# A float32 hybrid decoder layer: side transfers moved to the weights' queue, value blocks interleaved, PSUM banks tracked by the planner

## The chip, the cores and the metric

The kernel runs on one core of a Trainium2 chip. The metric is device time in microseconds (us), the median of three runs. The engines are named as in the profile: PE (TensorE, matmuls), PEld (its weight loads), DVE (VectorE), ACT (ScalarE), POOL (GpSimd) and SP (SyncE, which here only issues transfers). A q behind an engine's name (ACTq) is its sequencer: it issues transfers and waits, and stands in one line with the engine's own work.

## The reference

For 256 tokens of width 2048 the layer computes, in float32,

```python
h = rms_norm(x, norm_g)
proj = h @ dn_w_in                       # 2048 -> q, k, v, a/b gates, xq, z
q, k, v = silu(conv4(q)), silu(conv4(k)), silu(conv4(v))
mix = rms_norm(gated_delta_rule(l2(q), l2(k), v, g(a), sigmoid(b)))   # 24 value heads
xa  = softmax(rms_norm(xq) @ rms_norm(K).T / 16) @ V   # K, V = rms_norm(mem) @ mem_w_kv, 256 tokens
out = x + (concat(mix, xa) * silu(z)) @ w_out
```

The delta rule is done in chunks of 128 tokens here. For each chunk and head a unit lower triangular 128x128 matrix has to be inverted: `inverse` does the 32x32 diagonal blocks by substitution on DVE, `merge` joins them with small matmuls.

## The kernel before

**Weights.** All weight matrices come in 273 tiles of 128x1024 float32 (512 KB, named `st`, five buffers). Each is split into a rounded half `hi`, a cast on ACT (L261), and a rest `lo`, a subtraction on DVE (L263). The pair is a `wt` tile (four buffers), and every large product is done as hi*hi + hi*lo + lo*hi in the fast fp32r format. `wnext` traces transfer, cast and subtraction of one tile together; `wload` keeps `LOOK = 1` tile beyond the one in use.

**Products.** `proj_b` (tiles `pb`) makes 256x512 outputs from 8 or 16 weight tiles, in two PSUM banks, with 12 matmuls of 512 columns for each weight tile. `proj_a` (tiles `pa`) makes a 128-column block of projected features over 256 tokens from two weight tiles, one matmul of 512 and one of 256 columns for each of 16 k tiles. The eight PSUM banks are in groups: `pa` 2, `A` 2, `m` 2, `tr` 1, `B` 1.

**Order of the large work** (`PLAN`, L49 to 72): V0, V1 (values of the memory), K0, the gate columns `ab`, K1, then eight `x` blocks (queries of the cross-attention), `k` blocks with Z6 and Z7 (columns of z) between, Z0 to Z2, then for each of 12 head pairs a `q` and two `v` blocks with the remaining `k` and Z blocks between, and four output blocks `o`.

**Side work.** Everything else is written as Python generators. The program keeps a clock `now` that runs with the matmuls' estimated lengths, and resumes a generator when its estimated inputs are there: `mem_stats` and `tok_prep` (the two input norms; `tok_prep` makes the token tiles `hkt` that `ab` and everything from `x` on reads), `gates`, `decay`, `gram` (product `pkk`), `inverse`, `merge` (products `pm`), `delta` (`pkq`, `pvt`, `pU`, `pO`, `pqs`), `attend` (`xss`, `xsc`, `xpT`, `xo`) and `split_y` (transposes `pyT`). `calm` makes a generator wait while DVE has more than 0.8 us of estimated work. A scheduler then sorts the instructions of each engine again, by its own estimate of when each could start, with the traced order as priority. Nothing is pinned to the traced order. After that each engine is a strict queue.

**Transfers.** SP issues the weights, the inputs, the decay rows `erow` and the output. ACT issues what belongs to the inverses, through DRAM: each pair's matrix (`dN`), the diagonal blocks read back (`inN`), the inverted blocks written (`dY`, `dX`), and for each of six merges 6 loads into `XN` and 8 into `Y`. That is 84 loads of 16 KB for the six merges, and 27 more transfers.

**A finished product** of `proj_a` leaves its bank in two steps (`halves`, L309): ACT copies 256 columns, then DVE adds the other 256 from PSUM to them. A `Z` product is freed by the SiLU on ACT (`zs`).

Lines of helpers: L98 every side operation of DVE, ACT and POOL, L166 every matmul, L170 every transpose, L255 the weights' transfers.

Of the kernel before, what the change touches and what calls it, by code (L numbers as in the profile page):

```python
# [33 lines left out]
LOOK = 1  # L34
WARM = 7
XPACE = 1.5
HOP = 0.25
SLACK = 0.7
POLL = 0.3
CALM = 0.8  # L40
INV_CALM = 0.6
GATE_CALM = 0.8
# [6 lines left out]
PLAN = [("V", 0)] * 8 + [("V", 1)] * 8 + [("K", 0)] * 8 + [("ab", 0)] + [("K", 1)] * 8  # L49
# [30 lines left out]
def hybrid_kernel(ctx: ExitStack, tc: tile.TileContext, x, xT, memT, W, prm_d, cst_d, out):  # L80
    nc = tc.nc
    te, sy = nc.tensor, nc.sync
    now, fin = [0.0], [0.0]

    class Engine:
# [9 lines left out]
        def __getattr__(self, op):  # L95
            def call(*a, **k):
                self.run(self.cost(self, op, a, k))
                return getattr(self.eng, op)(*a, **k)  # L98
            return call
# [24 lines left out]
    po = Engine(nc.gpsimd, lambda e, op, a, k: 0.6)  # L124

# [33 lines left out]
    def mm(o_, lhsT, rhs, start, stop):  # L159
        n = 1  # L160
        for d in rhs.shape[1:]:
            n *= d
        if rhs.dtype == F32:
            n = 4 * max(n, 16)
        now[0] += n / 2400.0
        te.matmul(o_, lhsT, rhs, start=start, stop=stop)  # L166
# [59 lines left out]
    ahead = []  # L226
# [3 lines left out]
    def wnext():  # L230
        st = stp.tile([128, 1024], F32, name="st", tag="st")
        wt = wp.tile([128, 2, 1024], F32R, name="wt", tag="wt")
        hi, lo, src = wt[:, 0, :], wt[:, 1, :], st
        kind, t = PLAN[wpos[0]]
        if kind == "Z":
# [5 lines left out]
            hi, lo = [h.rearrange("p (k t c) -> p k t c", k=2, t=4) for h in (hi, lo)]  # L241
            src = st.rearrange("p (t k c) -> p k t c", t=4, k=2)
            dst = st.rearrange("p (t c) -> p t c", t=4)
        else:
            data, dst = W[plain[0]], st
            plain[0] += 1
        if kind == "ab":

            v = wt.rearrange("p a (k c) -> p (a k c)", c=64).rearrange("p (k a c) -> p k a c", a=2, c=64)
            hi, lo, src = v[:, :, 0, :], v[:, :, 1, :], st.rearrange("p (k c) -> p k c", c=64)  # L250
        parts = 2 if wpos[0] == 0 else 1
        dma[0] = max(dma[0], free.pop(0)) + 1.46
        for a in range(parts):
            w = slice(a * 1024 // parts, (a + 1) * 1024 // parts)
            sy.dma_start(dst[:, w] if parts > 1 else dst, data[:, w] if parts > 1 else data)  # L255
            if parts > 1:
                if a == 0:
                    sy.dma_start(prm[:, 0:P_CW], prm_d[:, 0:P_CW])
                mem_load(a, 1)
            se.run(0.95 / parts, dma[0] + 2.0)  # L260
            se.eng.copy(hi[:, w] if parts > 1 else hi, st[:, w] if parts > 1 else src)  # L261
            ve.run(1.14 / parts, se.end)
            ve.eng.tensor_tensor(out=lo[:, w] if parts > 1 else lo, in0=st[:, w] if parts > 1 else src,  # L263
                                 in1=hi[:, w] if parts > 1 else hi, op=ALU.subtract)
# [44 lines left out]
    def halves(dst, pt):  # L309

        se.copy(dst, pt[:, 256:512])
        yield
        ve.tensor_tensor(out=dst, in0=pt[:, 0:256], in1=dst, op=ALU.add)
        yield

    def proj_b(steps, act, tag, done, before=None):

        pts = [PS(tag, "pb0"), PS(tag, "pb1")]
        n = len(steps)
        for s in range(0, n, 2):  # L320
# [8 lines left out]
            for i, (r, k2) in enumerate(rk):  # L329
# [902 lines left out]
```

## Time and profile before

| | |
|---|---|
| median of three runs | 889.41 us (887.72 to 889.97) |
| the profiled execution: its time, its span | 890.17 us, 888.4 us |
| PE busy | 870.1 us, 98% of the span |
| DVE, ACT busy | 636.3 us (72%), 524.8 us (59%) |
| granted TensorE clock, mean | 0.996 |
| HBM read | 158.14 MB, 186 GB/s over the span |

The span is what lies between the first and the last instruction; 1.77 us of the profiled execution's time lie around it. Busy time of ACT does not hold the time in which it issues or waits for transfers. In the timeline a row is: start, length, engine, line, operation, out<-in, shape, count, and in brackets the idle time of the engine before it with what ended it.

### The profile page before, as it was taken

The numbers are of one execution on the slowest core, as the hardware profiler recorded it, in microseconds if no ns is written. First come the engines' busy times: TensorE is split into PE (matmuls) and PEld (weight loads), VectorE is DVE, ScalarE is ACT, GpSimd is POOL, SyncE is SP. The second block draws the span as 40 slices with busy tenths as digits, with TensorE's granted clock in tenths as the row PEclk, the third lists the DMA queues.
The fourth block names the chain that finished last, engine by engine and source line by source line (L and its number), as shares of the span: only waits on it lengthen the run. The fifth ranks groups of instructions, "written<-read, shape, count | busy, mean of one in ns | idle before, by whom it ended". The sixth has DMA issues, their size and how long they took to land.

```text
span 888.4 us, 13971 instructions
## 1 busy us (share of the span) xinstructions
PE 870.1 (98%) x5091; PEld 732.1 (82%) x5091; DVE 636.3 (72%) x1275; ACT 524.8 (59%) x936; POOL 45.9 (5%) x62
## 2 busy tenths in 40 slices
PE   8998999999999999999999999999999999999998
PEld 5886888888877788887888888878888888888886
DVE  6779886668784899976679998852878765454442
ACT  7655555577665655536589976555866754333341
POOL 0000000101010000121000001100000000000000
PEclk9998999999999999999999999999999999999999
DMA  8963555566767675676636555653544546766560
GB/s 287 345 209 122 186 168 150 174 203 206 240 214 207 212 239 189 194 207 184 186 114 187 178 175 176 170 180 104 166 137 138 166 154 230 231 191 224 199 204 25
DMA packets 98637, 165.90 MB, mean 187 GB/s; under 512 B 24304, under 2 KB 64008, under 8 KB 98568
## 3 DMA queue, kind: packets, MB, share of 16 engines
q1 hardware_dynamic: 72816, 158.08, 55.2%
q10 hardware_dynamic: 25752, 6.93, 3.3%
q8 instruction: 40, 0.66, 0.3%
q14 instruction: 29, 0.24, 0.1%
HBM read 158.14 MB, written 6.84 MB: 186 GB/s over the span
## 4 chain that ended last, share of the span: by engine, by line
PE 81%; DVE 6%; DMA 4%; ACT 3%; issue 3%; POOL 1%; ACTq 1%; SPq 0%; DVEq 0%; POOLq 0%
PE pb L166 43%; PE pa L166 29%; PE pO L166 2%; DVE wt L263 2%; DMA st<-W_d 2%; PE pm L166 1%; ACT wt L261 1%; PE pU L166 1%; PE pkq L166 1%; DVE acc L98 1%; PE xsc L166 1%; DMA erow<-dgc 1%; DMA XN<-dX 1%; PE xo L166 1%; PE pyT L170 1%
## 5 line engine op out<-in xcount | busy, mean ns | idle before, releaser
L263 DVE TENSOR_TENSOR wt<-st,wt 128x1024 fp32r<-128x1024 f32 (+1 forms) x274 | 332.4, 1216 | 125.0 <-ACT wt L261 122.5
L261 ACT CAST wt<-st 128x1024 fp32r<-128x1024 f32 (+1 forms) x274 | 285.7, 1047 | 192.0 <-PE pb L166 127.2
L166 PE MATMUL pa<-hkt,wt 128*128 128x512 f32 (+1 forms) x1792 | 336.5, 342 | 1.5 <-DVE wt L263 1.3
L166 PEld LDWEIGHTS pa<-hkt,wt 128*128 128x128 f32 x1792 | 274.1, 188 | 40.0 <-DVE wt L263 1.4
L166 PE MATMUL pb<-wt,hkt 128*128 128x512 f32 x768 | 183.9, 394 | 4.3 <-ACT zs L98 2.2
L166 PEld LDWEIGHTS pb<-wt,hkt 128*128 128x128 f32 x768 | 141.5, 188 | 35.4 <-ACT zs L98 3.5
L166 PE MATMUL pb<-wt,yhi 128*128 128x512 f32 x512 | 158.6, 391 | 0.0
L166 PEld LDWEIGHTS pb<-wt,yhi 128*128 128x128 f32 x512 | 95.2, 188 | 19.2
L166 PE MATMUL pb<-wt,ylo 128*128 128x512 f32 x256 | 99.7, 390 | 0.0
L166 PE MATMUL pb<-wt,mkt 128*128 128x512 f32 x384 | 94.2, 403 | 2.4 <-ACT mkt L98 0.9
L166 PEld LDWEIGHTS pb<-wt,mkt 128*128 128x128 f32 x384 | 74.1, 195 | 20.7 <-DVE wt L263 2.2
L98 DVE SCALAR_TENSOR_TENSOR acc<-raw,prm,acc 128x255 f32<-128x255 f32 x144 | 68.9, 479 | 9.3 <-ACT acc L98 8.3
L166 PEld LDWEIGHTS pb<-wt,ylo 128*128 128x128 f32 x256 | 48.0, 188 | 10.2
L98 ACT COPY raw<-pa 128x256 f32<-128x256 f32 x48 | 17.9, 373 | 35.5 <-PE pa L166 31.8
L98 ACT ACT_TABLE_LOAD x29 | 37.2, 1283 | 1.2 <-DVE acc L98 0.7
L98 DVE TENSOR_SCALAR dec<-erow,gcc 128x128 f32<-128x128 f32 x96 | 23.0, 279 | 18.2 <-DMA erow<-dgc 18.2
L98 DVE TENSOR_TENSOR inT<-inXT,inN 96x1 f32<-96x1 f32 (+22 forms) x92 | 29.9, 341 | 0.3
L98 DVE TENSOR_REDUCE inXT<-inT 96x1 f32<-96x1 f32 (+22 forms) x92 | 29.1, 337 | 0.4
L98 ACT ACTIVATE acc<-raw,prm 128x256 f32<-128x256 f32 x48 | 24.4, 509 | 7.8 <-DMA Y<-dY 3.8
L98 POOL TENSOR_TENSOR e<-e,mhalf 128x4 f32<-128x4 f32 x12 | 13.5, 1123 | 270.9 <-DVE e L98 270.9
L98 POOL TENSOR_TENSOR srk<-skt,mhalf 128x2 f32<-128x2 f32 x12 | 12.4, 1032 | 221.4 <-DVE skt L98 221.4
L98 DVE TENSOR_TENSOR raw<-pa,raw 128x256 f32<-128x256 f32 x48 | 20.1, 418 | 4.6 <-ACT raw L98 4.3
(199 smaller groups left out, 698.8 us busy)
## 6 DMA issues: line engine op xcount, KB each, us to landing
st<-W_d SPq DMA_DIRECT2D x272, 512.0 KB, 4.2
erow<-dgc SPq DMA_DIRECT2D x24, 256.0 KB, 4.4
dN<-dec ACTq DMA_DIRECT2D x12, 256.0 KB, 2.6
xraw<-xT_d SPq DMA_DIRECT2D x8, 256.0 KB, 5.4
res<-x_d SPq DMA_DIRECT2D x8, 256.0 KB, 4.6
mst<-memT_d SPq DMA_DIRECT2D x7, 256.0 KB, 4.5
out_dram<-res SPq DMA_DIRECT2D x7, 256.0 KB, 5.3
inN<-dN ACTq DMA_DIRECT2D x4, 192.0 KB, 4.1
```

What stands on the lines that cost most here:

```text
L98: return getattr(self.eng, op)(*a, **k)
L166: te.matmul(o_, lhsT, rhs, start=start, stop=stop)
L170: te.transpose(o_, i_, ident)
L261: se.eng.copy(hi[:, w] if parts > 1 else hi, st[:, w] if parts > 1 else src)
L263: ve.eng.tensor_tensor(out=lo[:, w] if parts > 1 else lo, in0=st[:, w] if parts > 1 else src, in1=hi[:, w] if parts > 1 else hi, op=ALU.su ...
```

## The change

1. **Side transfers.** All the transfers that ACT issued (`se.dma_start`) go through SP (`sd.dma_start`). ACT keeps three, at the very start: two pieces of the memory and the parameters.
2. **Weights.** `wnext` is split. `wraw` traces transfers for as long as one of the five `st` buffers is free by the planner's clock; `wnext` casts and subtracts. `LOOK` is 2. The memory pieces have their own buffers and no longer share `st`.
3. **Order.** V0 and V1 alternate tile by tile, so that a memory k tile serves both; then K0, K1, and `ab` behind K1. Z7 takes four tiles each after k3 and k4.
4. **Banks.** `PS`, `give`, `spare`, `bank` keep when each PSUM bank is free by the planner's clock; generators and products wait for it there. Z1 moves from the banks `A` to `pa`, x0, x1 and K1 change groups too, `ab` takes `B`.
5. **`halves`** copies all 512 columns in one ACT instruction; DVE adds the halves in SBUF.
6. **Traced order.** While the planner's clock is under 45 us every instruction is pinned behind the one traced before it on its engine.
7. **Estimates.** Small matmuls and transposes get other lengths; the three limits of `calm` double; `tok_prep` and `mem_stats` start at 8 us of the planner's clock (24 and 12 before), with 3.0 us per piece (1.5 before).

```diff
-LOOK = 1
+LOOK = 2
+PINNED = 45.0
-CALM = 0.8
-INV_CALM = 0.6
+CALM = 1.6
+INV_CALM = 1.2
-PLAN = [("V", 0)] * 8 + [("V", 1)] * 8 + [("K", 0)] * 8 + [("ab", 0)] + [("K", 1)] * 8
+PLAN = [("V", 0), ("V", 1)] * 6 + [("V", 0)] * 2 + [("V", 1)] * 2
+PLAN += [("K", 0)] * 8 + [("K", 1)] * 8 + [("ab", 0)]
...
+    def pin(ins):
+        return tc.keep_in_program_order(ins) if PINNED is None or now[0] < PINNED else ins
...
+    class Transfers:
+        def dma_start(self, *a, **k):
+            fin[0] = max(fin[0], now[0] + 3.0)
+            return sy.dma_start(*a, **k)
+    sd = Transfers()
...
+    def spare(tag, n=1):
+        return sum(t <= now[0] for t in idle[tag]) >= n
+    def give(pt, t):
+        idle[held.pop(id(pt))[0]].append(t)
+    def bank(tag, name):
+        yield from until(lambda: spare(tag))
+        return PS(tag, name)
...
+    def wnext():
+        while wpos[0] < len(PLAN) and free:
+            wraw()
...
-    def halves(dst, pt):
-        se.copy(dst, pt[:, 256:512])
-        yield
-        ve.tensor_tensor(out=dst, in0=pt[:, 0:256], in1=dst, op=ALU.add)
+    def halves(pt):
+        raw = S2("raw", [2, 256])
+        se.copy(raw.rearrange("p a t -> p (a t)"), pt)
+        give(pt, se.end)
+        yield
+        ve.tensor_tensor(out=raw[:, 0, :], in0=raw[:, 0, :], in1=raw[:, 1, :], op=ALU.add)
...
+        if kt < 2:
+            ve.tensor_scalar(out=m[:, 0, :], in0=src, scalar1=g, scalar2=None, op0=ALU.mult)
+        else:
+            se.activation(m[:, 0, :], src, AF.Copy, scale=g)
...
-                    se.dma_start(ys[p2][b, :, b], tsp[k][:, s0 : s0 + 4])
+                    sd.dma_start(ys[p2][b, :, b], tsp[k][:, s0 : s0 + 4])
...
-            return proj_b(kts, x_act, "pa" if 3 <= t < 6 else "A", z_done(t))
+            return proj_b(kts, x_act, "pa" if t in (1, 3, 4, 5) else "A", z_done(t))
-    spawn(mem_stats(), 12.0)
-    spawn(tok_prep(), 24.0)
+    first_loads()
+    spawn(mem_stats(), 8.0)
+    spawn(tok_prep(), 8.0)
```

What this makes of the engines' queues is seen at four places. First DVE at the start of the program. Before, with `gqk` (a product of two parameters), `wt` the rest of the first weight tile's two parts, and `mkt` the first memory tiles:

```order
L98 MEMSET warm 128x256
L98 TENSOR_TENSOR gqk<-prm 128x2
L263 TENSOR_TENSOR wt<-st,wt 128x512
L98 SCALAR_TENSOR_TENSOR mkt<-mst,prm,mkt 128x256
L263 TENSOR_TENSOR wt<-st,wt 128x512
```

And now, on the same engine:

```order
L112 MEMSET warm 128x256
L112 TENSOR_SCALAR nA<-nA 24x1
L112 TENSOR_SCALAR mkt<-mst,prm 128x256
L112 SCALAR_TENSOR_TENSOR mkt<-mst,prm,mkt 128x256
L330 TENSOR_TENSOR wt<-st,wt 128x512
L112 TENSOR_SCALAR mkt<-mst,prm 128x256
L112 SCALAR_TENSOR_TENSOR mkt<-mst,prm,mkt 128x256
L330 TENSOR_TENSOR wt<-st,wt 128x512
```

DVE now makes the rounded half of the first two memory tiles too, and ahead of all that stands `nA`, a small operation of `gates` that is traced late, is not pinned, and has come to the front. On ACT its input stands behind the casts of both parts of the first weight tile:

```order
L306 DMA mst<-memT_d 128x256
L308 DMA prm<-prm_d 128x40
L306 DMA mst<-memT_d 128x256
L326 ACT_TABLE_LOAD
L326 CAST wt<-st 128x512 x2
L112 ACTIVATE nA<-prm 24x1
L112 ACTIVATE msq<-mst 128x512
```

Second, PE from K0's end to the first x block. Before, K0 ends in pb_541 and pb_542 and K1 begins in pb_840 and pb_841; `pk` are the transposes of K0:

```order
L166 MATMUL pb_542<-wt,mkt 128x512 x6
L166 MATMUL pab<-hkt,wt 128x512 x8
L170 MATMUL pk<-cst,kn 128x128 x4
L166 MATMUL pab<-hkt,wt 128x512 x4
L170 MATMUL pk<-cst,kn 128x128 x2
L166 MATMUL pb_840<-wt,mkt 128x512
L170 MATMUL pk<-cst,kn 128x128 x2
L166 MATMUL pb_840<-wt,mkt 128x512
```

And now, at K1's end (pb_736 and pb_760; the transposes of K0 stand inside K1):

```order
L95 MATMUL pb_736<-wt,mkt 128x512 x6
L95 MATMUL pb_760<-wt,mkt 128x512 x6
L95 MATMUL pab<-hkt,wt 128x512 x14
L95 MATMUL pa<-hkt,wt 128x512
L95 MATMUL pa<-hkt,wt 128x256
L95 MATMUL pab<-hkt,wt 128x512
```

The gate columns stand behind K1, and 14 of their 16 matmuls follow each other.

Third, the loads of the first merge. Before, on ACT, between casts of weights and evictions (raw, acc, kq belong to blocks of k):

```order
L98 DMA XN<-dX_106 32x4x32
L98 ACTIVATE acc<-raw,prm 128x256
L98 DMA XN<-dX_106 32x4x32 x3
L98 COPY raw<-pa 128x256
L98 DMA XN<-dX_106 32x4x32 x2
L98 DMA Y<-dY_104 32x4x32
L98 ACTIVATE kq<-acc 128x256
L98 DMA Y<-dY_104 32x4x32 x2
L98 DMA dN_103<-dec 128x4x128
L98 DMA Y<-dY_104 32x4x32 x5
L98 ACTIVATE acc<-raw,prm 128x256
L261 CAST wt<-st 128x1024 x3
```

And now, on SP, between transfers of weights:

```order
L95 DMA st<-W_d 128x1024 x13
L95 DMA dY_104<-inXT 96x512 x2
L95 DMA st<-W_d 128x1024
L95 DMA dX_106<-inN 96x512
L95 DMA st<-W_d 128x1024 x3
L95 DMA XN<-dX_106 32x4x32 x6
L95 DMA Y<-dY_104 32x4x32 x8
L95 DMA st<-W_d 128x1024 x2
```

ACT has none of these left; 14 loads stand between two weights on SP.

Fourth, the first `pm` products on PE. Before:

```order
L166 MATMUL pkk<-kq 128x128
L166 MATMUL pm<-Y,dec 32x32 x16
L166 MATMUL pb_3832<-wt,hkt 128x512
L166 MATMUL pb_3831<-wt,hkt 128x512 x2
L166 MATMUL pb_3832<-wt,hkt 128x512 x2
L166 MATMUL pb_3831<-wt,hkt 128x512 x3
```

And now:

```order
L95 MATMUL pm<-Y,dec 32x32
L95 MATMUL pa<-hkt,wt 128x512
L95 MATMUL pa<-hkt,wt 128x256
L95 MATMUL pa<-hkt,wt 128x512
L95 MATMUL pm<-Y,dec 32x32
L95 MATMUL pa<-hkt,wt 128x256
...
L95 MATMUL pm<-Y,dec 32x32 x13
```

The first merge stands earlier, among the blocks of k and v instead of a Z block, and its first products come one by one between large matmuls. Over the whole program the number of runs of `pm` on PE goes from 29 to 39; the numbers of matmuls of every kind stay what they were.

More of the change, by code (lines that the diff above doesn't have):

```diff
@@ new lines, in wraw, with first_loads @@
+        wpos[0] += 1
+        raws.append((n, kind, st, src, dma[0] + 2.0))
+    def first_loads():
+        mst[0] = S2("mst", [512])
+        for a in range(2):
+            w = slice(a * 256, (a + 1) * 256)
+            pin(nc.scalar.dma_start(mst[0][:, w], memT[0][:, w]))
+            if a == 0:
+                pin(nc.scalar.dma_start(prm[:, 0:P_CW], prm_d[:, 0:P_CW]))
+    def wnext():
+        while wpos[0] < len(PLAN) and free:
+            wraw()
+        n, kind, st, src, landed = raws.pop(0)
+        wt = wp.tile([128, 2, 1024], F32R, name="wt", tag="wt")
+        hi, lo = wt[:, 0, :], wt[:, 1, :]
+        if kind == "Z":
+            hi, lo = [h.rearrange("p (k t c) -> p k t c", k=2, t=4) for h in (hi, lo)]
@@ L247, in wnext @@
         if kind == "ab":
             v = wt.rearrange("p a (k c) -> p (a k c)", c=64).rearrange("p (k a c) -> p k a c", a=2, c=64)
-            hi, lo, src = v[:, :, 0, :], v[:, :, 1, :], st.rearrange("p (k c) -> p k c", c=64)
-        parts = 2 if wpos[0] == 0 else 1
-        dma[0] = max(dma[0], free.pop(0)) + 1.46
+            hi, lo = v[:, :, 0, :], v[:, :, 1, :]
+        parts = 2 if n == 0 else 1
         for a in range(parts):
             w = slice(a * 1024 // parts, (a + 1) * 1024 // parts)
[L255 to L264, printed above, removed]
+            se.run(0.06 + 0.87 / parts, landed)
+            pin(se.eng.copy(hi[:, w] if parts > 1 else hi, st[:, w] if parts > 1 else src))
@@ L271, in wload @@
     def wload():
-        while wpos[0] < len(PLAN) and len(ahead) <= LOOK:
+        while (raws or wpos[0] < len(PLAN)) and len(ahead) <= LOOK:
             wnext()
@@ L711, in attend @@
         ve.tensor_tensor(out=pTl, in0=pp, in1=pTh, op=ALU.subtract)
+        give(pp, ve.end)
         yield from pe_soon()
-        px = PS("m", "xo")
+        px = yield from bank("m", "xo")
         c0 = (hd % 2) * 256
@@ L761, in gram @@
         kq, d = KQ[p], dD[p]
-        pk = PS("m", "pkk")
+        pk = yield from bank("m", "pkk")
         for b in range(NB):
@@ L946, in split_y @@
             yield from until(lambda: yf[j] is not None)
-            pt = PS("m", "pyT")
+            pt = yield from bank("m", "pyT")
             for h in range(2):
@@ L999, in delta @@
         se.activation(q2, kq[:, 1, :], AF.Square)
-        pk = PS("m", "pkq")
+        pk = yield from bank("m", "pkq")
+        vt = yield from bank("tr", "pvt")
         kqf = kq.rearrange("d a t -> d (a t)")
@@ L1025, in delta @@
         ve.tensor_tensor(out=kcl, in0=pkv[:, 0:4:2, :], in1=kch, op=ALU.subtract)
+        give(pk, ve.end)
         yield from pe_soon()
-        A = PS("A", "pU0")
+        A = yield from bank("A", "pU0")
         for h in range(2):
```

225 lines of the change are left out of this document (136 added, 89 removed).

## The prediction

> **What bounds the kernel now.** I read the page first, then windows of the engines' busy time, the chain of waits, the timeline of PE and of ACT at each gap, and the groups by form.
>
> ```profile
> span 888.4 us, 13971 instructions
> PE 870.1 (98%) x5091; PEld 732.1 (82%) x5091; DVE 636.3 (72%) x1275; ACT 524.8 (59%) x936; POOL 45.9 (5%) x62
> DVE  6779886668784899976679998852878765454442
> ```
>
> PE is idle for 888.4 - 870.1 = 18.3 us in all. The change leaves every matmul in place, so it can gain only those 18.3 us and the places where PE is busy but slow. DVE is full (nines) around slices 15 to 17 and 23 to 26, where the inverses and the delta rule run. From the chain of waits and from windows:
>
> ```profile
> 744.26 140.15 PE pb L166 x618
> ```
>
> ```profile
> 0.00:24.00 24.00, 20.37 (x67) 13.51 (x68) 17.04 (x32) 19.19 (x34) 0.20 (x4) 1.00 0.82 287
> 80.00:90.00 10.00, 7.80 (x25) 5.73 (x26) 8.87 (x22) 3.48 (x10) 0.00 (x0) 0.66 0.15 49
> ```
>
> The last 140 us are dense: 140.15 / 618 = 0.227 us for a matmul of 512 columns. No edit touches them. In the first 24 us PE runs 67 matmuls, 7 of them to warm up; 60 x 0.227 = 13.6, so 10.4 us are lost there. At 80 to 90 us PE does 25, at a granted clock of 0.66. Between these and the end, PE's timeline shows where it stands still:
>
> ```profile
> 77.26 1.98 PE L166 MATMUL pab<-hkt,wt 128*128 128x512 f32 x8
> 80.39 0.83 PE L170 MATMUL pk<-cst,kn 128*128 128x128 f32 x4 [1.15 <-DVE kn L98]
> ...
> 83.76 1.22 PE L166 MATMUL pab<-hkt,wt 128*128 128x512 f32 x2 [1.80 <-DVE hkt L98]
> ...
> 87.33 3.92 PE L166 MATMUL pb<-wt,mkt 128*128 128x512 f32 x13
> 91.10 0.39 PE L166 MATMUL pab<-hkt,wt 128*128 128x512 f32 x1
> ...
> 253.98 1.20 PE L166 MATMUL pb<-wt,hkt 128*128 128x512 f32 x4 [1.49 <-ACT zs L98]
> 276.87 1.43 PE L166 MATMUL pb<-wt,hkt 128*128 128x512 f32 x5 [0.38 <-ACT zs L98]
> 300.29 0.97 PE L166 MATMUL pb<-wt,hkt 128*128 128x512 f32 x3 [0.38 <-ACT zs L98]
> 401.16 0.50 PE L166 MATMUL pb<-wt,hkt 128*128 128x512 f32 x1 [1.34 <-ACT wt L261]
> ...
> 621.53 0.48 PE L166 MATMUL pa<-hkt,wt 128*128 128x512 f32 x1
> 621.94 0.26 PE L166 MATMUL pm<-Am,XN 32*32 32x32 f32 x8
> ...
> 623.92 1.32 PE L166 MATMUL pa<-hkt,wt 128*128 128x256 f32 x6 [1.28 <-DVE wt L263]
> 645.16 1.06 PE L170 MATMUL pyT<-cst,o 128*128 128x128 f32 x8 [1.14 <-DVE ylo L98]
> 671.99 0.63 PE L170 MATMUL pyT<-cst,o 128*128 128x128 f32 x4 [0.73 <-DVE ylo L98]
> ```
>
> So there are five kinds of loss: the start, the gate columns that wait for token tiles, Z products that wait for a bank, weights split too late around the merges, and transposes that wait for a bank.
>
> **The change part by part.**
>
> *Start.* The rows of before:
>
> ```profile
> 3.51 0.62 ACT L261 CAST wt<-st 128x512 fp32r<-128x512 f32 x1 [1.50 <-DMA st<-W_d]
> 4.76 0.51 ACT L98 ACTIVATE mkt<-mst,prm 128x256 fp32r<-128x256 f32 x1 [0.63 <-DMA mst<-memT_d]
> 5.32 5.41 PE L166 MATMUL pb<-wt,mkt 128*128 128x512 f32 x12 [0.93 <-ACT mkt L98]
> 5.62 0.62 ACT L261 CAST wt<-st 128x512 fp32r<-128x512 f32 x1 [0.36 <-DMA st<-W_d]
> 6.27 0.69 DVE L263 TENSOR_TENSOR wt<-st,wt 128x512 fp32r<-128x512 f32 x1 [0.49 <-ACT wt L261]
> 16.99 0.18 ACT L98 ACTIVATE nA<-prm 24x1 f32<-24x1 f32 x1
> ```
>
> The memory now travels beside the first weights, and each of its k tiles serves two weight tiles, so DVE and ACT have half the memory work per weight tile and the stops after the first tile should go. But `nA` is first on DVE, and on ACT its input stands behind the second cast. I put the second half of the first weight tile at 4.3 us (5.62 - 0.36 = 5.26 before, with two transfers fewer ahead of it; an estimate). Then both casts end at 4.9, `nA` on ACT and DVE (0.18, taken for both) at 5.3, the first rounded memory tile (taken as the 0.51 that it takes on ACT) at 5.8, its rest as much later at 6.3, the weights' rest (0.69) at 7.0. The first matmul starts at 5.8 instead of 5.32, the second waits until 7.0, and the first tile ends between 11.1 and 12.0 us, by when PE comes to its full rate (12 matmuls in 5.41 us before: half rate). That is 11.1 to 12.0 less 12 x 0.227 = 8.4 to 9.3 lost instead of 10.4. **Gain 1.5** (ends: -1 if the clock comes later, 3.5 if `nA` costs nothing).
>
> *Gate columns.* From 77.26 to 87.33 us PE does 14 `pab`, 2 `pb` and 8 transposes: 16 x 0.227 + 1.06 (eight transposes at 645.16) = 4.7 of 10.1 us, 5.4 lost; the next 13 matmuls take 3.77 instead of 2.95, since the clock has dropped, 0.8 more. Now `ab` stands behind K1, eight weight tiles (22 us) later, and `tok_prep` starts earlier. What is late next: the last two token tiles stand on ACT behind K1's squares and a cast.
>
> ```profile
> L98 ACT ACTIVATE junk<-pb 128x256 f32<-128x256 f32 x8 | 3.0, 380 | 1.6 <-PE pb L166 1.6
> L98 DVE TENSOR_TENSOR hkt<-hf,hkt 128x256 fp32r<-128x256 f32 x16 | 6.0, 418 | 0.0
> ```
>
> After K1 ends these are two squares (0.76), a cast (1.05), two casts of `hkt` (taken as 0.8) and two subtractions (0.84): 3.5 us, against 14 `pab` x 0.227 = 3.2 that are ready. I leave 0.8 for it. **Gain 5.4** (4 to 6.2).
>
> *Z banks.* Z0, Z1, Z2 took the same banks in turn; now Z1 has others, and Z7 ends a k block before Z0. The three waits on `zs` go: 1.49 + 0.38 + 0.38. What hides the SiLU then is a k block or another Z product. **Gain 2.2** (1 to 2.5).
>
> *Side transfers.* What an issue and a wait cost on ACT:
>
> ```profile
> L98 ACTq DMA_DIRECT2D XN<-dX x36: 309/434/643, 390.0 to 611.0; - x36
> ```
>
> ```profile
> L98 ACTq DMA_DIRECT2D Y<-dY x48: 309/442/1932, 395.1 to 617.2; - x48
> ```
>
> ```profile
> 617.70 1.14 ACT L98 ACTIVATE vs<-pvt,sV 128x128 f32<-128x128 f32 x4 [4.43 <-DMA Y<-dY]
> ```
>
> The merges' loads alone hold ACT for 36 x 0.434 + 48 x 0.442 = 36.8 us, in six bursts of 6.1 us, and with the waits in them ACT stands idle for up to 4.43 us at a time while casts are behind it. That is what PE's waits at 401.16 and 623.92 come from (1.34 + 1.28), and the transposes at 645.16 and 671.99 (1.14 + 0.73) follow the second. On SP a burst delays weights instead:
>
> ```profile
> L255 SPq DMA_DIRECT2D st<-W_d x274: 327/328/432, 0.7 to 862.3; - x137
> ```
>
> ```profile
> L263 DVE TENSOR_TENSOR wt<-st,wt 128x1024 fp32r<-128x1024 f32 (+1 forms) x274 | 332.4, 1216 | 125.0 <-ACT wt L261 122.5
> L261 ACT CAST wt<-st 128x1024 fp32r<-128x1024 f32 (+1 forms) x274 | 285.7, 1047 | 192.0 <-PE pb L166 127.2
> ```
>
> ```profile
> st<-W_d SPq DMA_DIRECT2D x272, 512.0 KB, 4.2
> erow<-dgc SPq DMA_DIRECT2D x24, 256.0 KB, 4.4
> ...
> Y<-dY ACTq DMA_DIRECT2D x48, 16.0 KB, 1.8
> ```
>
> Five buffers are 5 x 12 x 0.227 = 13.6 us of PE's work; landing (4.2), cast (1.05) and subtraction (1.22) leave 7.1 us, more than a burst of 6.1, so it stays hidden. **Gain 4.0** of the 4.5 us of waits (1 to 6).
>
> [...]
>
> *Weights five ahead.*
>
> ```profile
> ACT wt L261 <- DMA st<-W_d: 6.9, 7, 2.2
> ```
>
> Casts wait for a landing 6.9 us in all, and the first two rows of the start (1.50, 0.36) are in that; the scheduler sent transfers ahead as buffers came free anyway. Nothing, both ways up to 1.
>
> *One copy instead of copy and add.*
>
> ```profile
> L98 ACT COPY raw<-pa 128x256 f32<-128x256 f32 x48 | 17.9, 373 | 35.5 <-PE pa L166 31.8 <-DVE dec L98 3.2
> L98 ACT COPY xa<-xo 128x512 f32<-128x512 f32 x4 | 2.3, 586 | 8.8 <-PE xo L166 8.8
> ```
>
> ACT pays 57 x (0.586 - 0.373) = 12.1 us, much less than the 36.8 that leave it; DVE's add keeps its length (0.418 for `hkt`, in SBUF). The bank comes free one DVE step sooner. Hidden: zero, bounds 1 either way.
>
> *Merges in pieces.* The first products of a merge now stand singly between large matmuls, 10 more runs on PE. At 621.53 the step from a large matmul to a small one takes 0.41 us instead of 0.23: 10 x 0.18 = 1.8. **Cost 2** (1 to 4).
>
> *Merges earlier, on shorter notice.* ACT's evictions for the merges stand up to three weight tiles ahead of PE's, in more places than before, and by the count of matmuls ahead of it the first merge now begins some 40 us earlier, where DVE is full. No row shows these waits. Nearest from below is none; from above 1.3 us each (the waits at 401.16 and 623.92) for six merges, 8. I take **3** (2 for the merges, 1 for DVE).
>
> The sum: -1.5 - 5.4 - 2.2 - 4.0 + 2 + 3 = -8.1. The profiled execution took 890.17 us, 0.76 above the median of 889.41; so 882.1 against it, and 881.3 against the median.
>
> **The rivals.**
>
> *Side transfers wait behind weights.* On ACT's queue a load of 16 KB landed in 1.8 us; on SP's, `erow` among weights took 4.4. In one queue each merge's loads may come 2.6 us later than the order on PE assumes, and PE, a strict queue, stops at the first `pm`: 6 x 2.6 = 15.6, so 881.3 + 15.6 = 896.9, slower than before. It decides where PE reaches a merge less than 2.6 us behind the landing planned for it. For it: the singles of `pm` show that the plan has PE there as the loads land. Against: `erow` is sixteen times as large. [...]
>
> *The waits move.* The waits for weights around the merges go, but PE stops as long for evictions and a clogged DVE there. Then the 4.0 fall away, the other gains are 9.1, and the two costs stand between 8 together and their upper ends (4 and 8): 889.4 - 9.1 + 8 = 888.3 to 892.3, about the same. For it: DVE's nines; against it: ACT has 36.8 - 12.1 = 24.7 us less to do.
>
> *More than that comes back.* The PE steps that are slow but not idle around the merges also come from late splits; both costs vanish: 889.4 - 13.1 = 876.3, and with the upper ends of the start (3.5) and of the transfers (6) 872.3. For it: 401.16 is one of only two such waits that show as idle, yet ACT's bursts are six; against: most of a burst lay where casts were ahead.
>
> *The change does not do what it says* at the start: the pinned order holds there, but `nA` floated ahead of it. If that costs the whole gain and 1 us more, 883.8; this lies in the forecast's range.
>
> **How the numbers follow.** Forecast, 881.3 us, 874 to 888 where its terms' bounds do not all fall on one side: 0.55. More comes back, 872 to 876: 0.20. About the same, 888 to 892: 0.13. Slower by late transfers, 897: 0.12. The range 870 to 893 leaves out the last and little more. This kernel can be told from itself to about 0.3%, 2.7 us. Faster by more holds the forecast nearly whole (0.54), the third rival (0.20) and a little of the second (0.01): 0.75. Same: most of the second, 0.10. Slower: the first and the rest of the second, 0.15.
>
> **What would show it.** In the profile after: the first `pb` at about 5.8 us with a second stop near 7; no window at 80 to 100 us with a clock under 1, and at most 1 us of PE idle before the last `pab`; no wait of PE on `zs` over 0.3; no DMA-issue rows of XN and Y on ACT, and ACT's idle time before `vs`, `acc`, `kq` not ended by a DMA. Wrong would be: `pm` rows on PE with waits of 2 us and more ended by a DMA (the first rival), casts that wait for `st` beyond a total of 7 us (SP blocks weights), or a sum of PE's idle time that is again 18 us.

## The result, and the profile after

The changed kernel takes 878.50 us (median of 4 runs, 878.10 to 878.71) against 889.69 for the kernel before on the same chip: a ratio of 0.9872, 95% interval 0.9846 to 0.9898. The forecast was 881.3 us with a range of 870 to 893. The profiled execution took 878.10 us, 12.1 us less than that of before.

The page of the changed kernel, its first lines (busy time, share, instructions):

```profile
span 876.3 us, 13987 instructions
PE 866.8 (99%) x5091; PEld 731.9 (84%) x5091; DVE 639.4 (73%) x1277; ACT 539.8 (62%) x938; POOL 45.5 (5%) x62
```

PE's idle time fell from 18.3 to 9.5 us, and its busy time by 3.3, with the same matmuls: 8.8 us of standing still and 3.3 us of slow steps went. ACT is busy 15 us longer; what 11 of them are worth is tried below (old_halves).

PE, ACT and DVE at the start, from the timelines (start, length, and in brackets the idle time and what ended it):

```profile
4.50 1.38 ACT L326 CAST wt<-st 128x512 fp32r<-128x512 f32 x2 [1.08 <-DMA st<-W_d]
5.78 0.20 ACT L112 ACTIVATE nA<-prm 24x1 f32<-24x1 f32 x1
6.01 0.14 DVE L112 TENSOR_SCALAR nA<-nA 24x1 f32<-24x1 f32 x1 [4.85 <-ACT nA L112]
6.60 0.77 PE L95 MATMUL pb<-wt,mkt 128*128 128x512 f32 x1 [2.21 <-DVE mkt L112]
7.63 8.63 PE L95 MATMUL pb<-wt,mkt 128*128 128x512 f32 x31 [0.26 <-DVE wt L330]
```

The chain is the one that the prediction walked: casts, `nA` on ACT, `nA` on DVE, then the memory tile. It runs 0.6 to 0.8 us later than forecast; ACT's first cast waits for the weights until 4.50 us (3.51 before).

The same stretches by windows as before (engines in the order PE, PEld, DVE, ACT, POOL, then clock, DMA share, GB/s):

```profile
0.00:24.00 24.00, 20.30 (x74) 14.44 (x75) 18.02 (x32) 18.60 (x30) 0.20 (x4) 1.00 0.93 353
80.00:90.00 10.00, 10.00 (x48) 8.29 (x47) 9.97 (x19) 4.98 (x9) 0.00 (x0) 1.00 0.64 207
90.00:100.00 10.00, 10.00 (x48) 8.28 (x47) 7.54 (x15) 7.45 (x18) 0.31 (x1) 1.00 0.57 181
```

In the first 24 us PE gets through 74 matmuls instead of 67. The hole at 80 us is gone, and with it the dropped clock (1.00 granted at 80 to 90 us, 0.66 before). Of PE's list of waits these are left, besides the warm-up's (us in all, times, longest):

```profile
PE pb L95 <- DVE mkt L112: 2.2, 1, 2.2
PE pa L95 <- ACT zs L112: 1.2, 1, 1.2
PE pm L95 <- ACT Y L112: 0.6, 3, 0.2
PE pb L95 <- DVE wt L330: 0.3, 1, 0.3
```

No wait of `pm` on a DMA, none of `pab`, none of `pyT`. The second row is new: at 507 us a bank that Z3 used is asked for again by the next `pa`, and the SiLU is late. So the change removed waits on `zs` in one place and made one in another, and the prediction's sign "no wait of PE on `zs` over 0.3" failed there.

Landing times, from the DMA table (issues, size of each, median us from issue to landing):

```profile
st<-W_d SPq DMA_DIRECT2D x272, 512.0 KB, 4.0
Y<-dY SPq DMA_DIRECT2D x48, 16.0 KB, 1.7
XN<-dX SPq DMA_DIRECT2D x36, 16.0 KB, 3.1
```

And of XN before the change:

```profile
XN<-dX ACTq DMA_DIRECT2D x36, 16.0 KB, 4.1
```

In the weights' queue a load of Y lands in 1.7 us, on ACT's it took 1.8; XN 3.1 and 4.1. (It is not the queue that shortened XN: in act_transfers, below, it lands in 3.0 us on ACT's.) The first rival is refuted by these rows and by PE's list, where no `pm` waits for a DMA.

### The profile page after: what moved, and what is told of

It reads as the page before. It is cut to its first block, busy times and chain, and to the rows that moved or that the text cites. A ratio compares the mean times of both kernels' runs of the same rounds, so it can differ in the third digit from the quotient of the medians.

```text
span 876.3 us, 13987 instructions
## 1 busy us (share of the span) xinstructions
PE 866.8 (99%) x5091; PEld 731.9 (84%) x5091; DVE 639.4 (73%) x1277; ACT 539.8 (62%) x938; POOL 45.5 (5%) x62
## 4 chain that ended last, share of the span: by engine, by line
PE 97%; ACT 1%; DMA 0%; issue 0%; DVE 0%; SPq 0%; DVEq 0%; ACTq 0%
PE pb L95 50%; PE pa L95 36%; PE pO L95 2%; PE pm L95 2%; PE pkq L95 1%; PE pU L95 1%; PE pyT L95 1%; PE xsc L95 1%; PE xo L95 1%; PE pkk L95 1%; PE pvt L95 1%; PE pqs L95 0%; DMA st<-W_d 0%; PE pab L95 0%; ACT Y L112 0%
## 5 line engine op out<-in xcount | busy, mean ns | idle before, releaser
L95 PE MATMUL pb<-wt,hkt 128*128 128x512 f32 x768 | 182.0, 393 | 0.0
L95 PE MATMUL pb<-wt,mkt 128*128 128x512 f32 x384 | 90.6, 396 | 2.5 <-DVE mkt L112 2.2
L112 ACT COPY raw<-pa 128x512 f32<-128x512 f32 x56 | 32.7, 585 | 53.2 <-PE pa L95 53.1
L112 DVE TENSOR_TENSOR raw<-raw 128x256 f32<-128x256 f32 x57 | 23.9, 420 | 17.0 <-ACT raw L112 16.1
L112 POOL TENSOR_TENSOR e<-e,mhalf 128x4 f32<-128x4 f32 x12 | 16.5, 1372 | 302.7 <-DVE e L112 279.0
L112 DVE SCALAR_TENSOR_TENSOR o<-o,e,zs 128x128 f32<-128x128 f32 x48 | 14.3, 348 | 12.3 <-POOL e L112 12.2
```

Source lines behind the costliest of these rows:

```text
L95: return lambda *a, **k: pin(getattr(self.eng, op)(*a, **k))
L112: return pin(getattr(self.eng, op)(*a, **k))
```

## The experiments

All undo one edit in the changed kernel, add one to the kernel before, or alter the start. Each is compared with the kernel before on the same chip:

| run | median us | ratio to before, 95% interval |
|---|---|---|
| the change | 878.50 | 0.9872, 0.9846 to 0.9898 |
| act_transfers | 897.99 | 1.0102, 1.0075 to 1.0130 |
| cast1 | 888.48 | 0.9982, 0.9969 to 0.9994 |
| look1 | 885.02 | 0.9935, 0.9913 to 0.9957 |
| pin_PE | 882.41 | 0.9903, 0.9880 to 0.9925 |
| ab_early | 881.08 | 0.9910, 0.9888 to 0.9931 |
| Z1_on_A | 880.77 | 0.9908, 0.9885 to 0.9932 |
| nA_late | 879.79 | 0.9891, 0.9869 to 0.9913 |
| warm15_nA_late | 878.62 | 0.9875, 0.9854 to 0.9895 |
| old_halves | 878.07 | 0.9857, 0.9835 to 0.9880 |
| warm16 | 878.07 | 0.9867, 0.9846 to 0.9887 |
| before_SP | 888.07 | 0.9971, 0.9957 to 0.9986 |
| before_ab_late | 906.45 | 1.0183, 1.0163 to 1.0204 |

The medians of the kernel before itself, beside these runs, lie between 888.71 and 890.35 us; a difference of two rows below some 2 us is not told by the times alone, and then the traces are compared. "Slower" below is the difference of two medians that can come from different chips. By the ratios the differences to the changed kernel are 20.5 us (act_transfers), 9.8 (cast1), 5.6 (look1), 3.4 (ab_early), 3.2 (Z1_on_A) and 2.8 (pin_PE); the intervals of the last three overlap that of the change, so these rest on the traces.

Where traces are compared matmul by matmul, they are compared at points up to which PE has done the same matmuls in both.

The theory behind the prediction is that the edits' terms add up. The rival that the first run made likely: they are one plan, in which each edit is worth what the others let it be.

### Side transfers back on ACT (act_transfers)

```diff
-            return sy.dma_start(*a, **k)
+            return pin(nc.scalar.dma_start(*a, **k))
```

> The changed kernel with the side transfers (the merges' XN and Y loads, the inverses', the decays') issued on ACT's queue again; all else stays, so that ACT gets back the 84 issues of about 0.44 us. By the prediction's term the transfers were worth 4.0 us (1 to 6): 882.5 us (879.5 to 884.5), with PE idle again for 1 to 4 us behind casts or subtractions of the weights near 340 to 420 and 540 to 600 us, and ACT standing idle for some us at a time with a DMA as what ended it. The rival (the queue that issues hardly matters, and ACT's work beside it was hidden): 878.5 within 1 us, with the idle time of ACT back and none on PE. A second rival, that small loads are better off alone in a queue: 877 or less, with loads of Y that land 0.3 us or more sooner than the 1.7 us of the changed kernel.

19.5 us slower, outside all three. The loads are no quicker there (Y 1.7 us, XN 3.0). ACT and PE at the sixth merge, from the timelines:

```profile
586.20 4.81 ACTq L142 DMA_DIRECT2D Y<-dY  x8
589.85 0.57 PE L95 MATMUL pm<-Y,dec 32*32 32x32 f32 x4 [3.71 <-DMA Y<-dY]
591.05 1.04 ACT L326 CAST wt<-st 128x1024 fp32r<-128x1024 f32 x1 [6.08 <-DMA Y<-dY]
591.40 0.28 PE L95 MATMUL pm<-Y,dec 32*32 32x32 f32 x2 [0.98 <-DMA Y<-dY]
592.15 3.41 PE L95 MATMUL pb<-wt,hkt 128*128 128x512 f32 x7 [0.47 <-ACT wt L326]
```

The eight Y loads hold ACT's sequencer for 4.81 us and are issued late, since the XN loads and ACT's own work stand ahead (a copy of `u` that waits 1.90 us for DVE among it); PE comes to the merge and stops 3.71 us for them, then 0.98, then 0.47 for the cast that stood behind. After that its steps are slow (the seven matmuls of the last row take 3.41 us, 0.49 each), and the granted clock over 540 to 600 us is 0.91, where the changed kernel has 1.00:

```profile
540.00:600.00 60.00, 54.67 (x544) 43.51 (x543) 31.75 (x63) 33.44 (x89) 4.83 (x8) 0.91 0.41 116
```

Compared matmul by matmul with the trace of the changed kernel (PE's order is nearly the same), PE is 0.6 us behind ahead of the merges, 5.9 behind after three, 7.7 shortly before the sixth, 16.5 after it. So undoing the edit costs not 4.0 us but 16 to 20 in this order, half of it at one merge. What the prediction's term missed is not the issue itself but the loads' lateness: the planner's order counts on loads 3 us after they are asked for.

One thing is not as it was before. There the planner counted the 3 us from when ACT would be free, and booked 0.06 us of ACT for each issue; here it counts from its clock and books nothing. Part of the 16 to 20 us can therefore be a plan that does not know of ACT's queue. How much was not tried.

### The same edit alone in the kernel before (before_SP)

```diff
-        se.dma_start(...)
+        sd.dma_start(...)      # on SP, as in the change
```

> The kernel before with one edit, the side transfers issued on SP instead of ACT; weights, banks, merges and the place of the gate columns stay as they were. By the prediction's term 4.0 us go (1 to 6): 885 us against about 889 for before. A first rival, drawn from the run with the changed kernel's transfers back on ACT (19.5 us slower): ACT's bursts cost that much in any order, so 870. A second: with the old order most of a burst lay where casts were ahead, and the transfers are worth nothing without the merges' shorter notice: 889 within 1 us. A third, loads that come late behind weights: slower than before, with waits of PE at pm ended by a DMA.

0.9971 of before, 2.6 us by the ratio (1.2 to 3.8): inside the term's range, below its value, far from 19.5. But most of it is not where the term was. Matmul by matmul PE is 2.85 us ahead of the kernel before at the end of the profiled execution, and 2.25 of that it has by 331 us, before the first merge: 0.75 at 80 to 90 us, where the order of the engines is still the same as before, and 1.3 at the Z products. From the first merge on it gains 0.6. The two waits of PE for weights that the prediction named (401.16 and 623.92) are gone, but around the merges PE stops 0.86 us for `Am`, 0.85 for `oq` and 1.1 at `pyT`. (As with act_transfers, the planner's estimate of the landings changes with the edit.) Behind merges ACT's casts now wait for weights:

```profile
ACT wt L268 <- DMA st<-W_d: 13.1, 11, 3.5
```

Before the change this was 6.9 us in all, every wait of it in the first 36 us, and in the changed kernel it is 1.1. Here 7.1 us lie at the start and 6.0 between 300 and 650 us, where the merges are: in the old order the bursts on SP do hold up weights. In the changed kernel no such wait is left there. So the one term has two sizes: 0.6 us from the merges on in the old order (2.6 with what the run gained elsewhere), 16 to 20 when it is undone in the new one. That merges come closer behind their loads there fits the waits of PE on Y; it was not tried by itself.

### Weights and casts less far ahead (look1, cast1)

```diff
-LOOK = 2
+LOOK = 1
...
-        while wpos[0] < len(PLAN) and free:
+        while not raws or wpos[0] < min(8, len(PLAN)) and free:
             wraw()
```

Both edits in look1; the first alone in cast1.

> The changed kernel with a weight tile's transfer issued only as its cast is planned, and casts planned one tile ahead instead of two, as before the change (the first eight transfers stay as they are, for the memory travels with them). By the prediction five ahead is worth nothing, up to 1 us either way: 878.5 (877.5 to 879.5), with some waits more of casts for a landing. The rival: SP now issues the side transfers too, and only transfers issued early keep the weights out of their way: 3 us and more slower, with PE behind casts that wait for st around the merges.

> The changed kernel with casts planned one weight tile ahead instead of two, and the transfers still issued up to five tiles ahead. The run with both undone was 6.5 us slower; this one tells which of the two it was. If the transfers' early issue is what counts: 878.5 within 1 us here. If the casts' place in ACT's and DVE's order counts: 885, with waits of PE on wt and on what ACT does between casts (zs, vs) near 500 to 520 us.

look1 is 6.5 us slower, cast1 10.0. So the casts' place counts, not the transfers' issue: with casts one tile ahead, transfers five ahead do not help (cast1's casts wait 2.9 us in all for landings, look1's 4.3). That cast1 is even 3.5 us slower than look1 is not explained; the traces part by 2.8 us between 523 and 582 us. PE in cast1, from the timeline:

```profile
504.37 0.96 PE L95 MATMUL pb<-wt,hkt 128*128 128x512 f32 x3 [0.54 <-DVE wt L330]
...
508.80 0.75 PE L95 MATMUL pU<-vs,Y 128*128 128x128 f32 x4 [1.40 <-ACT vs L112]
...
511.48 10.97 PE L95 MATMUL pa<-hkt,wt 128*128 128x512 f32 x52 [1.30 <-ACT zs L112]
```

And the window around it, of the changed kernel and of cast1:

```profile
500.00:520.00 20.00, 18.77 (x108) 15.90 (x107) 19.88 (x42) 12.77 (x24) 3.52 (x2) 1.00 0.50 161
```

```profile
500.00:520.00 20.00, 16.73 (x80) 13.56 (x80) 18.08 (x39) 9.87 (x19) 5.90 (x7) 0.91 0.55 169
```

PE stops three times within 7 us, and the granted clock of the window is 0.91 (1.00 in the changed kernel's). A likely reason, argued and not tried: a cast (1.05) and a subtraction (1.22) are 2.3 of the 2.7 us that PE needs for a tile, and one tile ahead little else fits between. Up to 481 us cast1 has lost nothing to the changed kernel; at 507 it is 1.6 us behind and at 592 all of 8.2. The three stops are the largest behind the start, and in look1 they are the same. The planner's order of the merges and deltas changed along with the edit from 330 us on, and which of its steps costs the rest was not tried.

### Merges' first products in one run (pin_PE)

```diff
-    te, sy = Pinned(nc.tensor), Pinned(nc.sync)
+    te, sy = Ordered(nc.tensor), Pinned(nc.sync)   # PE pinned to the end
```

> The changed kernel with PE's own order as traced to the end of the kernel, all other engines as they are; it moves only the first products of the six merges, from singles between large matmuls back to one run of sixteen. By the prediction the singles cost 10 switches of 0.18 us, 2 us: 876.5 (875 to 877.5). The rival: the singles are there because each load lands by itself, and PE, made to take them in one run, stops until the last has landed: 1 us and more for each merge, 880 to 885, with a wait of PE or its weight loads at pm ended by a DMA. No change, 878.5 within 0.5: switches saved and waits gained are alike.

3.9 us slower: the rival, less than its price. The orders of DVE, ACT and SP stay nearly as they were; on PE some products of the deltas and the second steps of merges move along with the singles. PE at the first merge, here and in the changed kernel:

```profile
346.56 0.22 PE L99 MATMUL pm<-Y,dec 32*32 32x32 f32 x2 [1.00 <-DMA Y<-dY]
347.40 0.24 PE L99 MATMUL pm<-Y,dec 32*32 32x32 f32 x2 [0.63 <-DMA Y<-dY]
348.61 0.22 PE L99 MATMUL pm<-Y,dec 32*32 32x32 f32 x2 [0.96 <-DMA Y<-dY]
349.41 0.63 PE L99 MATMUL pm<-Y,dec 32*32 32x32 f32 x26 [0.59 <-DMA Y<-dY]
```

```profile
344.89 0.22 PE L95 MATMUL pm<-Y,dec 32*32 32x32 f32 x2
345.04 1.21 PE L95 MATMUL pa<-hkt,wt 128*128 128x512 f32 x5
346.17 0.24 PE L95 MATMUL pm<-Y,dec 32*32 32x32 f32 x2
```

In pin_PE the loads of Y land at 347.36, 347.90, 348.47, 348.76 and 349.37 us (as far as landings are recorded), 0.3 to 0.6 us apart, and PE takes its products two at a time between stops; in the changed kernel the pieces are PE working in between. The first merge loses 3.8 us and the next stops of this kind, at 383 to 386 us, 3.0; some of it comes back later, and 3.7 remain. At the other four merges PE does not stop for loads. The prediction booked the pieces as a cost of 2 us; they save 3.7.

### Gate columns between K0 and K1 again (ab_early), and behind K1 in the kernel before (before_ab_late)

```diff
-PLAN += [("K", 0)] * 8 + [("K", 1)] * 8 + [("ab", 0)]
+PLAN += [("K", 0)] * 8 + [("ab", 0)] + [("K", 1)] * 8
```

And the reverse of it in the other.

> The changed kernel with the gate columns put back between K0 and K1; K1's banks, the memory's k tiles and the early start of the token tiles stay. By the prediction the place of the gate columns is what gains: the 5.4 us come back (4 to 6.2): 883.9 us (882.5 to 884.7), with PE idle or at half rate for that long where pab stands. The rival: the token tiles start at 8 instead of 24 on the planner's clock now, so that they would be ready in time even there, and the place is worth nothing: 878.5 within 1 us.

> The kernel before with one edit, the gate columns behind K1. By the prediction's term 5.4 us go (4 to 6.2), if the token tiles are ready by then though they start as late as before: 884 against about 889. From the run of the changed kernel with the columns put back, 2.6 us slower, a rival: some 4.5 us are gained in that stage, and 2 to 3 are given back at the first three merges, because the decays and all that follows start 22 us later: 886.5. A third: with the late start the token tiles still are not ready behind K1, and it gains under 1 us: 888 to 889.

ab_early is 2.6 us slower, less than the 5.4. Its windows:

```profile
80.00:90.00 10.00, 8.13 (x35) 5.57 (x33) 10.00 (x27) 6.47 (x14) 0.00 (x0) 0.99 0.01 2
90.00:100.00 10.00, 9.87 (x37) 8.06 (x38) 8.99 (x15) 5.05 (x8) 0.00 (x0) 0.84 0.70 236
```

24 matmuls fewer than in the changed kernel's 20 us, 24 x 0.21 = 5 us: the stage's loss is there, as sized. But some of it comes back: matmul by matmul PE is 6.0 us behind the changed kernel until 340 us (0.7 of that from the start) and only 2.8 behind at 400, among the first merges. The gates, and what hangs on them, come earlier in ab_early; that this is why was not tried.

before_ab_late is 16.3 us slower by the ratio, outside all that was expected. PE in its timeline:

```profile
80.22 0.83 PE L170 MATMUL pk<-cst,kn 128*128 128x128 f32 x4 [2.96 <-DVE kn L98]
85.54 9.67 PE L166 MATMUL pb<-wt,mkt 128*128 128x512 f32 x35 [4.49 <-ACT hkt L98]
```

K1 stands directly behind K0 on the same two banks there, with nothing between to fill the time; PE waits 2.96 us for `kn`, and 4.49 for ACT, which has the casts of the token tiles ahead. In this stage it loses 3.2 us to the kernel before, where the term had 5.4 gained. The larger part comes later: from 401 to 482 us it loses 12.4 us more, where PE stops for loads of Y and its granted clock is 0.66 (460 to 480 us):

```profile
462.81 0.22 PE L166 MATMUL pm<-Y,dec 32*32 32x32 f32 x2 [1.48 <-DMA Y<-dY]
466.21 0.63 PE L166 MATMUL pm<-Y,dec 32*32 32x32 f32 x26 [2.11 <-DMA Y<-dY]
```

```profile
460.00:480.00 20.00, 16.22 (x165) 13.38 (x164) 10.82 (x28) 12.63 (x33) 0.00 (x0) 0.66 0.48 149
```

So by itself the move is a loss. In the changed kernel K1 has other banks and the token tiles start earlier, and the waits for `kn` and `hkt` are gone there; which of the two it takes, and what spares the changed kernel the 12.4 us at the merges, no run shows.

### Z1 on the old banks (Z1_on_A)

```diff
-            return proj_b(kts, x_act, "pa" if t in (1, 3, 4, 5) else "A", z_done(t))
+            return proj_b(kts, x_act, "pa" if 3 <= t < 6 else "A", z_done(t))
```

> The changed kernel with Z1 on the banks that Z0 and Z2 use, as before the change. By the prediction the three waits on zs come back, 2.2 us (1 to 2.5): 880.7 us. From the trace of the changed kernel the stretch from 240 to 340 us gained more than that, some 4 to 5 us: if Z1's bank is the cause of all of it, 883. The rival: the planner now keeps account of the banks and puts its own hold there, which lets side work run instead of PE stopping, so nothing comes back: 878.5 within 1 us.

2.3 us slower by the medians. Two waits of 0.38 us on `zs` are back, and matmul by matmul PE loses 1.4 us from 245 to 320 us. The rest of the 2.3 lies within what the start does (below). That 1.4 and 2.3 lie about the term of 2.2 is no proof of it: the edit undoes only Z1's bank, two of the term's three waits, 0.76 of its 2.25 us. The third, 1.49 before Z0, goes with Z7's new place, which no run undid. The 4 us and more that I read from the whole stretch were more than Z1.

### The old way of adding halves (old_halves)

```diff
-        se.copy(raw.rearrange("p a t -> p (a t)"), pt)
-        give(pt, se.end)
+        se.copy(raw[:, 0, :], pt[:, 256:512])
         yield
-        ve.tensor_tensor(out=raw[:, 0, :], in0=raw[:, 0, :], in1=raw[:, 1, :], op=ALU.add)
+        ve.tensor_tensor(out=raw[:, 0, :], in0=pt[:, 0:256], in1=raw[:, 0, :], op=ALU.add)
+        give(pt, ve.end)
```

> The changed kernel with the old way of adding the two halves of a projection: ACT copies one half of the bank, DVE adds the other half out of the bank, which comes free after DVE. ACT does 12.1 us less. By the prediction one copy is worth nothing, up to 1 us either way: 878.5 (877.5 to 879.5). The rival: a bank that waits for DVE stops PE where DVE is full (waits of PE's pa on DVE's raw), 2 us and more slower; or ACT's 12 us are on the path, and it is 1 to 3 us faster.

878.07 us: no difference that can be told, as forecast. ACT is busy 528.7 us instead of 539.8, and those 11 us were hidden.

### The start (nA_late, warm16, warm15_nA_late)

```diff
-P_NG, P_MG, P_GQ, P_GK, P_GO, P_AL, P_DT, P_CW = 0, 16, 32, 34, 36, 37, 38, 40
+P_NG, P_MG, P_GQ, P_GK, P_GO, P_DT, P_CW, P_AL = 0, 16, 32, 34, 36, 38, 40, 232
```

```diff
-WARM = 7
+WARM = 16
```

The first edit is nA_late, the second warm16; the third run has the first edit and `WARM = 15`.

> The changed kernel with the column of a_log moved behind the convolution's weights, so that it comes with the second load of the parameters; on DVE the operation nA then stands behind the first seven tiles of weights and no longer first. By the prediction nA costs DVE a wait for ACT's second cast: the first pb starts some 0.5 us sooner (6.1 instead of 6.60 us), the second stop moves from 7.63 to about 7.1, and the time falls by 0.5 us (0.3 to 1.0): 878.0. The rival: the full rate of PE comes at the same moment whatever the start, so that the sooner matmuls run at half rate and half of it is lost: 878.25; or the parameters land only at 5.5 us and nothing changes: 878.5. All of this is below what can be told by the time alone; the trace of the first 12 us decides.

> The changed kernel with 16 matmuls to warm up instead of 7; the order of all other instructions stays. In the runs so far the first matmuls of the memory take 427 ns each until PE's rate doubles, at 10.3 us in the changed kernel, at 12.8 with nA late, at 15.3 in one run and at 10.9 and 11.3 in two others, with no tie to when the first one starts; 8 to 16 slow ones cost 0.2 us each. Theory: PE's rate follows its activity of the last microseconds, and the 2.2 us without work before the first pb put it back to the half; with warm-up matmuls up to the second stop at 7.6 us it is at its full rate from then: 1.6 us less than the changed kernel, 876.9 (876 to 877.5), and less spread between runs. The rival: the doubling comes so many microseconds after the first matmul of the memory, whatever ran before: 878.5; and the warm-ups, if they run past 7.6 us, cost up to 1 us: 879.5.

> The changed kernel with 15 matmuls to warm up and nA late, the two edits of the start together. Alone, the warm-ups gave 0.4 us (878.07) and nA late, though its first pb came 0.64 us sooner, was 1.3 us slower (879.79). Theory: nA late lost only because PE's rate doubled 2.5 us later in it; with PE kept busy that falls away, and DVE's chain at the start, which is the bound with a fast PE, is 0.6 us shorter: 877.4 (877.0 to 877.8), the first pb at 6.6 to 7.0 us, and no pb of 427 ns after 8 us. The rival: nA behind the first weight tiles costs something else, later: 878.8 to 879.8 with the start as fast as with 16 warm-ups.

With `nA` late the first `pb` starts at 5.96 instead of 6.60 us and the second stop ends at 6.99, as forecast; and after 20 matmuls PE is 0.9 us behind the changed kernel. The windows of 8 to 12 us, changed kernel first:

```profile
8.00:10.00 2.00, 2.00 (x5) 1.30 (x5) 2.00 (x3) 2.00 (x3) 0.00 (x0) 1.00 1.02 393
10.00:12.00 2.00, 2.00 (x9) 1.65 (x8) 2.00 (x5) 2.00 (x5) 0.00 (x0) 1.00 1.05 413
```

```profile
8.00:10.00 2.00, 2.00 (x6) 1.21 (x5) 1.81 (x3) 2.00 (x4) 0.00 (x0) 1.00 1.02 397
10.00:12.00 2.00, 2.00 (x6) 1.63 (x5) 2.00 (x4) 2.00 (x4) 0.00 (x0) 1.00 1.04 406
```

No wait explains it: PE's matmuls follow each other at 0.427 us until 10.3 us in the one and until 12.8 in the other, then at 0.227. With 16 warm-ups PE is never idle for long and the rate doubles while they run, from 0.427 to 0.217 us at 6.9 us (at 5.7 with 15 warm-ups and `nA` late); from the 20th matmul on PE is 0.5 us ahead of the changed kernel. That is less than the 1.6 us of slow matmuls that went, for with a fast PE DVE's subtraction is next:

```profile
9.12 11.18 PE L95 MATMUL pb<-wt,mkt 128*128 128x512 f32 x48 [0.41 <-DVE wt L330]
```

Both edits together are 0.8 us ahead after 20 matmuls, so nA's loss at the start was PE's rate, as the theory had it. But between 85 and 200 us both kernels with `nA` late lose some 0.5 us that no wait in the trace explains, and 878.62 is no better than 878.50. In the two runs whose matmuls kept running the rate doubled sooner, at 6.9 and 5.7 us instead of 10.3 and 12.8; the prize forecast for it did not come, and whether `nA`'s new place costs the 0.5 is open. The quickest versions, warm16 and old_halves at 878.07, are below the changed kernel by less than can be told.

In two runs the rate also went back. In pin_PE and old_halves, with 7 warm-ups and the same 2 us without work, the matmuls from 7.5 us on follow each other at 0.34 and 0.25 us, and behind the next stop at 0.427 again until 11.2 and 11.6 us. So in these two the half rate is not simply what the idle time just before left behind. The window of pin_PE:

```profile
8.00:10.00 2.00, 1.83 (x5) 0.95 (x5) 2.00 (x4) 2.00 (x4) 0.00 (x0) 0.51 1.01 381
```

## Why the prediction came out right, point by point

The forecast was 2.8 us too slow, and the first rival (slower than before) was wrong, as shown by the landing rows. The two traces show where the time went. At each point of this table PE has done the same matmuls in both; the last column is what the changed kernel gained since the point above.

| up to | PE there before, now (us) | forecast gain | gain |
|---|---|---|---|
| the end of K0 (start) | 77.26, 75.60 | 1.5 | 1.7 |
| the first x block (gate columns) | 110.48, 102.73 | 5.4 | 6.1 |
| a k block ahead of Z0 | 240.78, 231.66 | 0 | 1.4 |
| inside Z2 (Z banks) | 302.25, 289.02 | 2.2 | 4.1 |
| the last matmul (from the merges on) | 884.00, 872.08 | 4.0 - 2 - 3 = -1.0 | -1.3 |

The miss lies ahead of the merges: 13.2 us were gained there and 9.1 booked. From there on the net came out as forecast, a loss of 1.3 us against 1.0: the lead is 13.2 us at 350 us of the trace before, 11.6 at 468, and 10.5 at 542, behind the new wait on `zs`. But the three terms of that net were not right one by one, as the runs above show; that their sum was is partly luck.

- **Start, gain 1.5.** 10.4 us were lost in the first 24, now 24 - 67 x 0.227 = 8.8: a gain of 1.6 in the profiled execution. The chain was right and 0.6 to 0.8 us too early. Landing times were taken from before, when less was in flight (253 GB/s at 2 to 6 us, 305 now); that this is the reason was not tried. That the gain came out is partly luck: by the rate's doubling the same start did 62 matmuls in 24 us in one execution, 71 to 74 in the others.
- **Gate columns, gain 5.4.** The stage gained 6.1, near the term's upper end: no `pab` waits, so that the 0.8 held back for late token tiles was not needed. With the edit undone PE does 72 matmuls in 20 us instead of 96. Net of later stages undoing it costs 2.6. And it is no edit by itself (16.3 us slower alone, most of it at the merges). The prediction named the token tiles only as what would be late next, and K1's banks not at all.
- **Z banks, gain 2.2.** The three waits went, and the stretch gained 4.1: the waits of 2.25, one of 0.67 us for a weight at 288.97 before, and slow steps around them. Undoing Z1's bank alone brings back 1.4. Not foreseen was the new wait of 1.2 us behind Z3.
- **Side transfers, gain 4.0.** Mis-sized. It was read off the waits on PE in the old order; there the edit alone gains 2.6 us, and only 0.6 of it from the merges on, since other waits take the place of those that go. In the new order undoing it costs 19.5. Loads of Y land no sooner on one queue than on the other (1.7 us on either, in the changed kernel and in act_transfers); their issue on ACT takes 0.44 us for a load that lands in 1.7, and 4.81 for eight of them in a row.
- **Weights five ahead, 0.** Right for the transfers, as far as tried: with casts one tile ahead, issuing them later costs nothing. But `LOOK` also sets how far casts run ahead of PE, which the prediction did not see: that undone costs 10.0 us, with both undone 6.5.
- **One copy, 0.** Right.
- **Merges in pieces, cost 2.** Wrong in sign: 3.7 us saved. The pieces were priced as switches on PE; what PE would do otherwise, wait for the loads, was not.
- **Merges earlier, cost 3.** Not tried by itself. The traces show 0.6 us of waits of PE on `Y` for all merges. The prediction read DVE as full in slices 23 to 26; its row has nines in 15 to 17 and 22 to 24.

The third rival, that more comes back, gave 876.3 us, nearer to 878.5 than the forecast. But it rests on both costs vanishing around the merges, a gain of 4.0 there, and the table shows a loss of 1.3.

Undoing single edits costs 19.5, 10.0, 3.9, 2.6 and 2.3 us, more than three times the 11.2 of the whole. So the gains are a joint one, and what each edit is worth depends on the others; which of them makes up for which at the merges stays open. A sum of terms read from the old trace prices each edit in the old plan.

## What to carry over

Where a planner sets the order, price an edit in the order that it will stand in: for each wait that you book, ask what the strict queue would do without the edit there, as with the pieces of a merge, which look like switches and are a way not to wait. An edit that is worth 3 us alone can cost 19.5 when it is undone in the new plan, so undo edits in the new kernel as well as adding them to the old one. And compare traces at points up to which the same work is done: that tells in which stretch a gain lies, where a total can agree by chance. Ahead of a strict queue, the distance in work (casts two tiles ahead) counted for more here than the distance of transfers.

## What the runs showed of the hardware

- At the start PE's matmuls of 512 columns followed each other at 427 ns until the rate doubled: 2.6 us after they began to follow one another in the changed kernel (10.25 us less 7.63), 5.8 us after with `nA` late (12.75 less 6.99). In warm16, where PE had worked since 1.2 us, it came at 6.9, 5.7 us after. What sets the moment no run shows. With `nA` late the first `pb` came 0.64 us sooner and the doubling 2.5 us later, and after 20 matmuls PE was 0.9 us behind. The granted clock in the windows stood at 1.00 in several of these slow stretches (8 to 10 us in the changed kernel) and at 0.51 in a like one of pin_PE, so there it is the spacing of matmuls that tells.
- In three windows with several stops of 0.5 to 4 us the granted clock was lower: 0.91 (540 to 600 us in act_transfers, 500 to 520 in cast1) and 0.66 (460 to 480 in before_ab_late). A single stop of 1.23 us in the changed kernel (500 to 520 us) and one of 1.49 in the kernel before (250 to 260) left it at 1.00.
- The 16 KB loads of Y landed as fast among the weights' transfers as on ACT's queue (a median of 1.7 us in the changed kernel, 1.8 before, 1.7 in act_transfers); each held the sequencer that issued it for 0.43 us on SP and 0.44 on ACT (medians).
